# SwiGLU block products: weight sums formed by accumulating DMAs, another order of the 28 steps, unsplit value products, the last block by token tile

## The chip, the cores and the metric

One core of one Trainium2 chip runs one program, a whole decoder layer. The metric is the device time of one execution in microseconds (us). Names of the engines in the rows: PE is TensorE's matmul side and PEld its weight loads, DVE is VectorE, ACT is ScalarE, POOL is GpSimd, SP is SyncE, which here only issues transfers. SPq, ACTq and POOLq are the queues of DMA issues of those engines.

## What is computed

A layer on 512 tokens of width 2048, float32 in and out. The change touches the last two sublayers and one product of the first stage; the mixer ahead of them is left as it was.

```python
xa = _memory_cross_attention(h, mem, w_xq[l], w_xk[l], w_xv[l], w_xo[l])
h = _layer_norm(DEEPNORM_ALPHA * h + xa, ln2_g[l], ln2_b[l])
ff = (jax.nn.silu(h @ w_ffn_gate[l]) * (h @ w_ffn_up[l])) @ w_ffn_down[l]
h = _layer_norm(DEEPNORM_ALPHA * h + ff, ln3_g[l], ln3_b[l])
```

w_ffn_gate and w_ffn_up are 2048 x 5632, w_ffn_down is 5632 x 2048. The cross attention has 4 heads of 512 over 256 memory tokens.

## The kernel before, in words

**Precision.** A float32 product is made of three matmuls on rounded halves: a value x is stored as hi (x rounded to the matmul's type) and lo (x minus hi). hi is a cast on ACT, lo a subtract on DVE. Every weight tile goes through this pair once, every activation operand too.

**Seven products for eight.** The FFN runs as 2x2 block products by Strassen and Winograd's scheme, with 7 products P1 to P7 for 8. For gate and up there are 11 blocks j = 0 to 10 (512 output columns of gate and of up each): B11 and B21 are the two row halves of the gate columns, B12 and B22 those of the up columns, and the left operands are sums of quarters of the activations. For down there are 6 blocks: groups of 4, 4 and 3 of the gate/up blocks, two column halves each. A product is cut along the contraction into chunks c (4, or 3 in the last group), so a block has 28 steps, the last two blocks 21. One step (mm_item, L1298 to L1307) is 12 matmuls of 128x512 with one weight tile of 256x512.

**The feed of weights.** Class Feed prepares the weight tile of each step ahead of time. pump (L1142) lets SP load a 512 KB block tile into T0 to T3 or into one of four tiles rt. a (L1152 to L1154) subtracts two weight blocks on DVE where the product needs a sum (L1152), takes a tile ws (three of them) and casts the sum into its hi half on ACT (L1154). b (L1161) forms the lo half on DVE and frees the tiles that were used up. product_block calls after() behind each step: a for the step three ahead, b for the one two ahead, then pump. A block needs 20 loads of 512 KB and 16 subtracts at L1152 in gate/up.

**Order.** plan holds the order of the steps: P1 four times, P5 four times, then P6, P7, P3 for each chunk, then P2, P4 for each chunk. Each engine takes its instructions in the order in which the program issues them. Work beside the products (the elementwise part of a block, transposes, layer norms) is written as generators; sched advances them by one yield at each tick().

**Between blocks.** on() takes the products from PSUM with adds on DVE (L1333) and copies on ACT. ff_out transposes silu(gate)*up (L1342), forms the sums and differences for the down product (sums, L1040 to L1044; L1445 is the product ahead of the transposes), splits them (L1356 on ACT, L1360 on DVE) and sends them to comb_d in HBM by 16 small DMAs that ACT issues. load_comb brings them back for the down blocks.

**Ahead of the FFN.** wo_task (L534 to L539) multiplies the memory's values by w_xo; split_psum (L245, L246) splits each product into hi and lo, and POOL's DMA stores both to vo_d. At the output projection of the cross attention ("xo" below) next_w reloads the split halves as weights: whi and wlo, each by DMA. ln2 (L1010) and the transposes in first_half and second_half (L1053 in second_half) then build the seven activation operands. y2n_d keeps the normalised activations for the residual, which residual_task (L1293, L1294) turns into the term added behind the down product.

**The end.** In the last down block P4 is held back and done by token tile, so that final_ln (L1484 to L1493: DVE, ACT and POOL) can start on one tile while PE works on the next.

Of the kernel before, what the change touches and what calls it, by code (L numbers as in the profile page):

```python
# [9 lines left out]
F32 = mybir.dt.float32  # L10
F32R = mybir.dt.float32r
# [28 lines left out]
def layer_kernel(tc, x, mem, positions, ln_in_g, ln_in_b, w_in, sgu_norm_g, sgu_norm_b,  # L40
# [148 lines left out]
    def w_split(c):  # L189
# [192 lines left out]
    vo_d = [[dramp.tile([P, 2, 4, 512], F32R, name=f"vo_d{kb}_{cb}") for cb in range(4)] for kb in range(2)]  # L382
# [147 lines left out]
    def vo_chunk(h, cb):  # L530
        wh, wl = next_w(f"vo{h}_{cb}", 0)
        for mt in range(2):
# [440 lines left out]
    def zt(i, dt=F32):  # L973
        return pf[1].tile([P, 512], dt, name=f"z{i}")

    class Pieces:
        def __init__(self, where):
            self.t = {k: zt(i) for k, i in where.items()}

        def __getitem__(self, key):  # L980
            return self.t[key]
# [5 lines left out]
    comb_d = [dramp.tile([P, 7, 2, 256], F32R, name=f"comb_d{q}") for q in range(22)]  # L987
    comb = {}
    PS1, PS2, PS3, PS4, PA12, PA22, PA11 = range(7)

    def new_comb(p):
        if p == PA11 or p == PA12:
            comb[p] = [pf[0].tile([P, 4, 2, 256], F32R, name=f"c{p}_{h}") for h in range(2)]
        elif p == PS1 or p == PS2:
            comb[p] = [bigp.tile([P, 4, 2, 256], F32R, name=f"big{2 * (p == PS2) + h}") for h in range(2)]
        else:
            nm = {PS3: "wraw", PS4: "whi", PA22: "wlo"}[p]
            comb[p] = [wp.tile([P, 4, 2, 256], F32R, name=nm, bufs=2) for h in range(2)]

    def cslot(p, q, hl):  # L1000
        return comb[p][q // 4][:, q % 4, hl]
# [15 lines left out]
    def cm(i):  # L1017
        return pf[0].tile([P, 512], F32, name=f"cm{i}")

    def first_half():  # L1020
        for k in range(KT):
            p = aux()
            for t in range(2):
                T.transpose(p[:, t * 128:(t + 1) * 128], y2[t, k // 4][:, (k % 4) * 128:(k % 4) * 128 + 128], ident)
            g, b = cols[:, L2G + k:L2G + k + 1], cols[:, L2B + k:L2B + k + 1]
            pr = PA11 if k < 8 else PA12
            hi, lo = cslot(pr, k % 8, 0), cslot(pr, k % 8, 1)
            hf = cm(k % 4)[:, 0:256]
            A.activation(hi, p[:, 0:256], AF.Identity, bias=b, scale=g)
            if k % 2:  # L1030
                A.activation(hf, p[:, 0:256], AF.Identity, bias=b, scale=g)
            else:
                V.tensor_scalar(hf, p[:, 0:256], g, b, op0=OP.mult, op1=OP.add)
            V.tensor_tensor(lo, hf, hi.bitcast(F32), OP.subtract)
            if k % 2:
                yield 1

    def sums(xx, yy, ss, dd):
        a11, a21, a12, a22 = xx[:, 0:256], xx[:, 256:512], yy[:, 0:256], yy[:, 256:512]
        s1, s2, s3, s4 = ss[:, 0:256], ss[:, 256:512], dd[:, 0:256], dd[:, 256:512]  # L1040
        V.tensor_tensor(s1, a21, a22, OP.add)
        V.tensor_tensor(s2, s1, a11, OP.subtract)
        V.tensor_tensor(s3, a11, a21, OP.subtract)
        V.tensor_tensor(s4, a12, s2, OP.subtract)  # L1044
        return s1, s2, s3, s4

    def second_half():
        for q in range(8):
            m = []
            for n, k in enumerate((q, q + 8)):  # L1050
                p = aux()
                for t in range(NT):
                    T.transpose(p[:, t * 128:(t + 1) * 128], y2[t, k // 4][:, (k % 4) * 128:(k % 4) * 128 + 128],  # L1053
                                ident)
                g, b = cols[:, L2G + k:L2G + k + 1], cols[:, L2B + k:L2B + k + 1]
                m.append(cm(3 - n))
                A.activation(m[n], p, AF.Identity, bias=b, scale=g)
            ss, dd = cm(0), cm(1)
            s1, s2, s3, s4 = sums(m[0], m[1], ss, dd)
            src = ((PS1, s1), (PS2, s2), (PS3, s3), (PS4, s4), (PA22, m[1][:, 256:512]))  # L1060
            for pr, s in src:
                A.copy(cslot(pr, q, 0), s)
            for pr, s in src:
                V.tensor_tensor(cslot(pr, q, 1), s, cslot(pr, q, 0).bitcast(F32), OP.subtract)
            yield 1
        res_ready[0] = True


    class Feed:
        def __init__(self):  # L1070
            self.items, self.loads = [], []
            self.nl = self.na = self.nb = self.pos = 0
            self.rt = []
            self.T = {}

        def block(self, aps, n, order):
            T_, R = {}, {}
            base = len(self.items)

            def load(kind, c, tag, key):  # L1080
                self.loads.append((len(self.items), kind, aps[kind](c), tag, key))

            def add(name, c):
                e = dict(key=(name, c))
                if name == "P1":
                    load("B11", c, ("T", c), (base, "T", c))
                    e["src"] = (base, "T", c)
                elif name == "P5":
                    load("B12", c, ("r",), (base, "r5", c))
                    e["op"] = ((base, "T", c), (base, "r5", c), (base, "T", c))  # L1090
                    e["src"] = (base, "T", c)
                    e["free"] = [(base, "r5", c)]
                elif name == "P6":
                    load("B22", c, ("r",), (base, "r1", c))
                    e["op"] = ((base, "T", c), (base, "r1", c), (base, "T", c))
                    e["src"] = (base, "T", c)
                elif name == "P7":
                    load("B12", c, ("r",), (base, "r2", c))
                    e["op"] = ((base, "r2", c), (base, "r1", c), (base, "r2", c))
                    e["src"] = (base, "r2", c)  # L1100
                    e["free"] = [(base, "r2", c)]
                elif name == "P3":
# [503 lines left out]
```

## Time and profile before

| | us |
|---|---|
| three runs | 2755.64, 2749.66, 2753.16 |
| their median | 2753.16 |
| the profiled execution | 2757.52 |
| its span | 2755.8 |

| stage, us of the span | length | steps in it |
|---|---|---|
| the cross attention's keys, values and value products: 0 to 307.2 | 307.2 | |
| mixer, and the cross attention up to xo: 307.2 to 1182.5 | 875.3 | |
| xo with ln2: 1182.5 to 1305.5 | 123.0 | |
| gate/up block 0: to 1413.1 | 107.6 | 28 |
| gate/up blocks 1 to 10: to 2258.0 | 844.9 | 280 |
| first down block: to 2354.9 | 96.9 | 28 |
| next four down blocks: to 2657.8 | 302.8 | 105 |
| last down block: to 2729.4 | 71.6 | 21 |
| last layer norm: to 2755.8 | 26.4 | |

The profiled execution took 1.7 us more than its span and 4.4 us more than the median of the runs. PE is busy in 95% of the span, DVE in 68%, ACT in 39%, POOL in 4%; the granted clock is 0.98 of full speed over the whole.

### The profile page before, as it was taken

How to read it: one execution, taken by the hardware profiler on the slowest of the kernel's cores; microseconds unless marked ns; L12 is line 12 of the kernel's file. 1: busy time of each engine (PE TensorE's matmuls, PEld its weight loads, DVE VectorE, ACT ScalarE, POOL GpSimd, SP SyncE). 2: the span in 40 equal slices, each digit the busy share in tenths (PEclk: the TensorE clock that was granted, in tenths of full speed). 3: DMA queues.
4: the chain of work that ended last, by engine and by line, in shares of the span. 5: the costliest groups of instructions: out<-in, count | busy, mean ns of one | idle time of the engine just before them, and what ended most of it. 6: DMA issues, size and time to landing. Idle time of an engine off the chain costs nothing.

```text
span 2755.8 us, 32085 instructions
## 1 busy us (share of the span) xinstructions
PE 2609.4 (95%) x12453; PEld 2160.1 (78%) x12453; DVE 1869.7 (68%) x2520; ACT 1076.7 (39%) x1440; POOL 111.2 (4%) x141
## 2 busy tenths in 40 slices
PE   8999999999999999998899999999999998999994
PEld 8998888888888888876677777777777776878873
DVE  4777656463554366324788788887778777778888
ACT  4454333232331242202644444544445443333332
POOL 1311000000000010001100000000000000000004
PEclk9999999999999999999899999999999999999997
DMA  8879732323253234179465566555555687574642
GB/s 288 249 238 318 231 92 77 92 77 107 77 185 106 92 107 168 61 284 354 122 190 180 180 206 186 186 183 176 164 187 157 203 285 264 199 282 163 258 160 76
DMA packets 302040, 496.65 MB, mean 180 GB/s; under 512 B 17344, under 2 KB 111296, under 8 KB 299840
## 3 DMA queue, kind: packets, MB, share of 16 engines
q1 hardware_dynamic: 240048, 413.52, 45.1%
q10 hardware_dynamic: 46032, 47.46, 5.4%
q0 software_dynamic: 15808, 33.63, 3.8%
q8 instruction: 98, 1.61, 0.2%
q14 instruction: 54, 0.44, 0.0%
HBM read 412.22 MB, written 82.31 MB: 179 GB/s over the span
## 4 chain that ended last, share of the span: by engine, by line
PE 29%; DVE 13%; DMA 8%; ACT 3%; issue 3%; ACTq 1%; SPq 0%; DVEq 0%
PE acc L1306 6%; PE acc L1307 6%; PE acc L1305 6%; DVE ws L1161 4%; PE D L1306 3%; PE D L1307 3%; PE D L1305 3%; ACT ws L1154 2%; DVE T L1152 2%; DVE z L1333 2%; DMA comb_d<-z 2%; DMA wlo<-vo_d 1%; DMA rt<-in_w_ffn_gate_dram 1%; DVE z L1360 1%; DMA rt<-in_w_ffn_down_dram 1%
## 5 line engine op out<-in xcount | busy, mean ns | idle before, releaser
L1154 ACT CAST ws<-T 128x1024 fp32r<-128x1024 f32 x264 | 277.2, 1051 | 457.2 <-DVE T L1152 215.8
L205 DVE TENSOR_TENSOR wlo<-wraw,whi 128x1024 fp32r<-128x1024 f32 x226 | 267.1, 1223 | 219.5 <-ACT whi L204 219.5
L1161 DVE TENSOR_TENSOR ws<-T,ws 128x1024 fp32r<-128x1024 f32 x264 | 321.6, 1220 | 90.2 <-ACT ws L1154 88.3
L204 ACT CAST whi<-wraw 128x1024 fp32r<-128x1024 f32 x226 | 226.0, 1049 | 286.4 <-PE acc L242 175.0
L1161 DVE TENSOR_TENSOR ws<-rt,ws 128x1024 fp32r<-128x1024 f32 x198 | 240.9, 1220 | 77.4 <-ACT ws L1154 69.7
L1154 ACT CAST ws<-rt 128x1024 fp32r<-128x1024 f32 x198 | 205.4, 1052 | 186.7 <-PE acc L1307 66.2
L1152 DVE TENSOR_TENSOR T<-rt,T 128x1024 f32<-128x1024 f32 x198 | 241.0, 1217 | 9.7 <-DMA rt<-in_w_ffn_down_dram 9.7
L1306 PE MATMUL acc<-ws,big 128*128 128x512 f32 x528 | 214.8, 407 | 26.2 <-DVE ws L1161 25.7
L1305 PE MATMUL acc<-ws,big 128*128 128x512 f32 x528 | 212.5, 402 | 8.9 <-ACT ws L1154 6.7
L1306 PE MATMUL acc<-ws,c 128*128 128x512 f32 x512 | 203.1, 397 | 9.5 <-DVE ws L1161 8.4
L1307 PE MATMUL acc<-ws,big 128*128 128x512 f32 x528 | 210.0, 398 | 0.0
L1305 PE MATMUL acc<-ws,c 128*128 128x512 f32 x512 | 203.0, 397 | 0.8 <-ACT ws L1154 0.8
L240 PE MATMUL acc<-whi,act 128*128 128x512 f32 x512 | 201.2, 393 | 0.0
L1307 PE MATMUL acc<-ws,c 128*128 128x512 f32 x512 | 200.7, 392 | 0.0
L241 PE MATMUL acc<-wlo,act 128*128 128x512 f32 x512 | 199.4, 389 | 0.2 <-DVE wlo L205 0.2
L242 PE MATMUL acc<-whi,act 128*128 128x512 f32 x512 | 199.3, 389 | 0.0
L240 PE MATMUL acc<-act,whi 128*128 128x512 f32 x384 | 152.1, 396 | 0.0
L1306 PEld LDWEIGHTS acc<-ws,big 128*128 128x128 f32 x528 | 101.7, 193 | 62.0 <-DVE ws L1161 42.1
L242 PE MATMUL acc<-act,wlo 128*128 128x512 f32 x384 | 149.8, 390 | 0.0
L241 PE MATMUL acc<-act,whi 128*128 128x512 f32 x384 | 149.6, 390 | 0.0
L240 PE MATMUL acc<-memT,whi 128*128 128x256 f32 x432 | 125.4, 290 | 8.0 <-DVE vT L246 5.1
L1305 PEld LDWEIGHTS acc<-ws,big 128*128 128x128 f32 x528 | 101.5, 192 | 34.6 <-ACT ws L1154 10.1
(303 smaller groups left out, 5676.3 us busy)
## 6 DMA issues: line engine op xcount, KB each, us to landing
rt<-in_w_ffn_up_dram SPq DMA_DIRECT2D x132, 512.0 KB, 4.4
rt<-in_w_ffn_down_dram SPq DMA_DIRECT2D x88, 512.0 KB, 4.9
wraw<-in_w_in_dram SPq DMA_DIRECT2D x40, 1024.0 KB, 5.4
comb_d<-z ACTq DMA_DIRECT2D x132, 256.0 KB, 3.4
rt<-in_w_ffn_gate_dram SPq DMA_DIRECT2D x48, 512.0 KB, 4.8
T<-in_w_ffn_gate_dram SPq DMA_DIRECT2D x44, 512.0 KB, 3.8
wraw<-in_w_xv_dram SPq DMA_DIRECT2D x16, 1024.0 KB, 7.4
wraw<-in_w_xo_dram SPq DMA_DIRECT2D x16, 1024.0 KB, 6.6
```

Of the source, the lines that this page charges most:

```text
L204: A.copy(hi[s], r[:, z])
L205: V.tensor_tensor(lo[s], r[:, z], hi[s].bitcast(F32), OP.subtract)
L240: T.matmul(o, lh, rh, start=start, stop=False)
L241: T.matmul(o, lh, rl, start=False, stop=False)
L242: T.matmul(o, ll, rh, start=False, stop=stop)
L1152: V.tensor_tensor(o, x, y_, OP.subtract)
L1154: A.copy(e["ws"][:, 0], self.tiles[e["src"]])
L1161: V.tensor_tensor(e["ws"][:, 1], self.tiles[e["src"]], e["ws"][:, 0].bitcast(F32), OP.subtract)
L1305: T.matmul(banks[i], lh, rh, start=start and kk == 0, stop=False, skip_group_check=True)
L1306: T.matmul(banks[i], lh, rl, start=False, stop=False, skip_group_check=True)
L1307: T.matmul(banks[i], ll, rh, start=False, stop=kk == 1, skip_group_check=True)
L1333: V_ADD = lambda o, a_, b_: V.tensor_tensor(o, a_, b_, OP.add)
```

## The change

**Weight sums by DMA (gate/up).** Feed.block now gives each step a source tile and what is to happen to that tile behind the step's lo half ("post"). A tile X is loaded with B11 (gate) and serves P1; then POOL issues a DMA that adds B12 (up) onto it in place, and it serves P5; then one adds B22 (up) for P6, and one adds B21 (gate) for P4. Y is loaded with B22, serves P3, and gets B12 added for P7. Z is B21 for P2. So SP makes 12 loads of a block in place of 20, and POOL issues 16 accumulating DMAs of 512 KB. In the down blocks the sum for P6 is one DVE add for each chunk (the "add" in post), the rest is as in gate/up. Signs that the sums no longer carry are moved into the activation operands (L5, L6, L7, L3, A12, A22, A11).

**Order and ring.** Steps go by ORD; ws has four tiles; after() calls b ahead of a; on() comes behind after(). PSUM banks alternate in pairs. a is four steps ahead of PE's step, and b three ahead.

**Elementwise work in larger tiles.** to_features, ff_first and ff_second replace ff_out: casts and subtracts of 2 to 4 tiles of 512 at a time, comb_d stored by four DMAs of SP. residual_task runs in blocks 1 to 4. second_half goes by pairs with 32 transposes in place of 64, and block 0 waits for each chunk of the operands apart (gate). The operands of the next down group are loaded as each product of the block ahead ends.

**Value products unsplit.** wo_task copies the product to SBUF in float32 by one ACT copy, and POOL stores half the bytes; xo reloads one float32 tile of 1 MB in place of two split ones, and splits it like the other weights (2 casts of ACT and 2 subtracts of DVE for each of 16 chunks; L199 and the line behind it).

**Last block.** P7 and P4 stand last and go by token tile; tokens 0 and 1 are complete behind P6, step 15 of 21. The last two weight tiles of ws go into tiles of their own.

**The scratch of POOL's descriptors** is 1024 in place of 4096.

```diff
         def a(self):
...
-            if "op" in e:
-                o, x, y_ = (self.tiles[k] for k in e["op"])
-                V.tensor_tensor(o, x, y_, OP.subtract)
-            e["ws"] = pf[0].tile([P, 2, 1024], F32R, name="ws", bufs=NW)
+            if e["extra"]:
+                e["ws"] = pf[0].tile([P, 2, 1024], F32R, name=e["extra"])
+            else:
+                e["ws"] = pf[0].tile([P, 2, 1024], F32R, name="ws", bufs=NW)
             A.copy(e["ws"][:, 0], self.tiles[e["src"]])
...
             V.tensor_tensor(e["ws"][:, 1], self.tiles[e["src"]], e["ws"][:, 0].bitcast(F32), OP.subtract)
+            for act_ in e["post"]:
+                if act_[0] == "add":
+                    x_, y_ = self.tiles[act_[1]], self.tiles[act_[2]]
+                    V.tensor_tensor(x_, x_, y_, OP.add)
+                elif act_[0] == "acc":
+                    t = self.tiles[act_[1]]
+                    G.dma_start(t.rearrange("p (k c) -> p k c", k=2),
+                                act_[2].rearrange("(k p) c -> p k c", p=P), accum_op=OP.add)
...
         def after(self):
+            self.b()
             self.a()
-            self.b()
             self.pump()

-    NR, NW = 4, 3
+    NR, NW = 4, 4
...
+    head = lambda n: seq("P1", n) + seq("P2", n) + seq("P5", n)
+    ORD = {4: head(4) + its("30 60 31 61 32 33 62 70 63 71 72 73 40 41 42 43"),
+           3: head(3) + its("30 31 60 32 61 62 70 71 72 40 41 42")}
...
-            kv = p0.tile([P, 2, 512], F32R, name="vst", bufs=3)
-            split_psum(kv, p)
-            G.dma_start(vo_d[h // 2][cb][:, :, (h % 2) * 2 + mt], kv)
+            kv = p0.tile([P, 512], F32, name="vst", bufs=3)
+            A.copy(kv, p)
+            G.dma_start(vo_d[h // 2][cb][:, (h % 2) * 2 + mt], kv)
...
-    nc = _bacc.Bacc("TRN2", target_bir_lowering=False, num_devices=1, dynamic_dma_scratch_size=4096)
+    nc = _bacc.Bacc("TRN2", target_bir_lowering=False, num_devices=1, dynamic_dma_scratch_size=1024)
```

**Where instructions moved: the feed of a gate/up block.** DVE before, in the second half of a block: L1152 is a weight sum, L1161 a lo half, T2 and T3 are block tiles, rt the ring of four.

```order
L1161 TENSOR_TENSOR ws_14952<-rt_14815,ws_14952 128x1024
...
L1152 TENSOR_TENSOR rt_14907<-rt_14882,rt_14907 128x1024
L1161 TENSOR_TENSOR ws_14978<-T2_14611,ws_14978 128x1024
L1161 TENSOR_TENSOR ws_15000<-rt_14907,ws_15000 128x1024
L1152 TENSOR_TENSOR T3_14644<-rt_14955,T3_14644 128x1024
L1161 TENSOR_TENSOR ws_15015<-rt_14882,ws_15015 128x1024
L1152 TENSOR_TENSOR rt_14981<-rt_14955,rt_14981 128x1024
L1161 TENSOR_TENSOR ws_15041<-T3_14644,ws_15041 128x1024
L1161 TENSOR_TENSOR ws_15059<-rt_14981,ws_15059 128x1024
```

DVE now, in the middle of a block (L1166 is a lo half, L1323 an add out of PSUM):

```order
L1166 TENSOR_TENSOR ws_13093<-T0_12851,ws_13093 128x1024
L1166 TENSOR_TENSOR ws_13112<-T1_12872,ws_13112 128x1024
L1323 TENSOR_TENSOR Xa_13054<-D_10193,Xa_13054 128x512
L1323 TENSOR_TENSOR Xa_13054<-D_10194,Xa_13054 128x512
L1166 TENSOR_TENSOR ws_13130<-T2_12903,ws_13130 128x1024
L1166 TENSOR_TENSOR ws_13152<-T3_12922,ws_13152 128x1024
L1166 TENSOR_TENSOR ws_13168<-rt_13031,ws_13168 128x1024
L1166 TENSOR_TENSOR ws_13184<-T0_12851,ws_13184 128x1024
```

POOL now, in the same block; in the blocks of before its queue holds none of these:

```order
L1173 DMA T2_12903<-in_w_ffn_up_dram 128x2x512
L1173 DMA T3_12922<-in_w_ffn_up_dram 128x2x512
L1173 DMA rt_13031<-in_w_ffn_up_dram 128x2x512
L1173 DMA T0_12851<-in_w_ffn_gate_dram 128x2x512
L1173 DMA rt_13077<-in_w_ffn_up_dram 128x2x512
L1173 DMA T1_12872<-in_w_ffn_gate_dram 128x2x512
```

The weight sums are gone from DVE's row and stand in POOL's queue, each behind the lo half that last read its tile.

**ACT in xo.** Before, ACT has the normalisation (L1010) and first_half's work (L1029, L1031; c_0 and c_1 are operand tiles) in one run:

```order
L1010 ACTIVATE z_9520<-z_9520,mv 128x512
L1010 ACTIVATE z_9524<-z_9524,mv 128x512
L1010 ACTIVATE z_9521<-z_9521,mv 128x512
L1010 ACTIVATE z_9525<-z_9525,mv 128x512
L1029 ACTIVATE c_0_9796<-aux,cols 128x256 x2
L1031 ACTIVATE cm_9833<-aux,cols 128x256
```

Now (L199 is the cast of a value-product tile, L1016 the normalisation, L1040 and L1044 first_half):

```order
L199 CAST whi<-wraw 128x1024 x14
L1016 ACTIVATE Xb<-Xb,mv 128x512
L1016 ACTIVATE XH<-XH,mv 128x512
...
L199 CAST whi<-wraw 128x1024 x2
L1040 ACTIVATE Xb<-aux,cols 128x256 x2
L1044 CAST c_0_9763<-Xb 128x512
...
L199 CAST whi<-wraw 128x1024 x2
L1040 ACTIVATE Xb<-aux,cols 128x256 x2
```

The casts that make xo's weights now stand in ACT's queue between and behind the norm and first_half's work.

## Rows read from the trace of the kernel before

**Rows 1.** Stretches: start:end, length, busy of each engine (instructions), PEclk, DMA share, GB/s.

```profile
0.00:307.20 307.20, 290.11 (x2017) 272.19 (x2018) 204.04 (x288) 148.93 (x205) 50.30 (x73) 0.99 0.86 274
1182.52:1305.54 123.02, 107.07 (x474) 85.61 (x472) 41.41 (x95) 21.37 (x42) 7.29 (x12) 0.94 0.91 335
1305.54:1413.11 107.57, 94.52 (x402) 73.81 (x401) 87.62 (x150) 61.63 (x97) 8.34 (x12) 0.92 0.46 140
1413.11:2258.02 844.91, 806.15 (x3522) 644.86 (x3520) 686.95 (x768) 399.87 (x501) 0.00 (x0) 1.00 0.59 188
2258.02:2354.94 96.92, 84.08 (x354) 65.09 (x352) 71.62 (x82) 35.49 (x42) 0.00 (x0) 0.98 0.78 268
2354.94:2657.77 302.83, 293.13 (x1261) 237.69 (x1260) 240.24 (x243) 110.11 (x105) 0.00 (x0) 0.99 0.60 214
2657.77:2729.40 71.63, 61.94 (x253) 48.28 (x251) 65.55 (x84) 24.44 (x25) 9.56 (x7) 0.93 0.32 113
2729.40:2755.80 26.40, 0.16 (x1) 0.00 (x0) 22.54 (x32) 3.04 (x4) 18.24 (x14) 0.56 0.37 139
```

**Rows 2.** Waits of PE, then of ACT, in 1413.11:2258.02: us in total, times, longest.

```profile
PE acc L1306 <- DVE ws L1161: 20.9, 32, 1.4
PE aux L1342 <- DVE z L1445: 11.2, 20, 1.4
...
ACT ws L1154 <- DVE T L1152: 94.6, 42, 3.9
```

**Rows 3.** PE's timeline, one step of a gate/up block: start, length, [idle before, releaser].

```profile
1669.97 0.39 PE L1305 MATMUL acc<-ws,c 128*128 128x512 f32 x1
...
1672.69 0.38 PE L1342 MATMUL aux<-ident,z 128*128 128x128 f32 x2
1673.85 0.33 PE L1342 MATMUL aux<-ident,z 128*128 128x128 f32 x1 [0.78 <-DVE z L1445]
```

**Rows 4.** Groups by line and form in 1413.11:2258.02: busy us, mean ns, idle before.

```profile
L1161 DVE TENSOR_TENSOR ws<-T,ws 128x1024 fp32r<-128x1024 f32 x160 | 195.1, 1219 | 62.5 <-ACT ws L1154 61.0
L1152 DVE TENSOR_TENSOR T<-rt,T 128x1024 f32<-128x1024 f32 x120 | 146.1, 1217 | 0.0
L1152 DVE TENSOR_TENSOR rt<-rt 128x1024 f32<-128x1024 f32 x40 | 48.7, 1217 | 0.0
L1333 DVE TENSOR_TENSOR z<-D,z 128x512 f32<-128x512 f32 x40 | 27.5, 689 | 9.7 <-PE D L1307 9.2
...
L1154 ACT CAST ws<-T 128x1024 fp32r<-128x1024 f32 x160 | 168.0, 1050 | 242.6 <-DVE T L1152 94.6 <-PE acc L1307 66.1 <-DMA comb_d<-z 57.6
```

**Rows 5.** DMA in 1413.11:2258.02: a queue's packets, MB, share; issues, KB each, us to landing.

```profile
q1 hardware_dynamic: 63725, 121.81, 45.2%
...
rt<-in_w_ffn_up_dram SPq DMA_DIRECT2D x116, 512.0 KB, 4.5
```

**Rows 6.** POOL's issue of the vo_d stores, then (whole run) their landing.

```profile
L539 POOL DMA_DIRECT2D vo_d<-vst x32: 684/685/793, 76.4 to 312.3; - x32
```
```profile
vo_d<-vst POOLq DMA_DIRECT2D x32, 512.0 KB, 7.8
```

**Rows 7.** Wait for ACT at the vo_d split, PE's waits in xo, first L1010.

```profile
ACT vst L245: 21.8, 6
```
```profile
PE acc L241 <- DMA wlo<-vo_d: 13.6, 8, 4.4
```
```profile
1246.12 0.81 ACT L1010 ACTIVATE z<-z,mv 128x512 f32<-128x512 f32 x1 [48.87 <-DVE mv L390]
```

**Rows 8.** Waits of PE in block 0.

```profile
PE aux L1053 <- ACT cm L1057: 8.3, 5, 2.8
```

**Rows 9.** Timelines of DVE, POOL and PE in the last down block.

```profile
2717.92 0.22 DVE L272 SCALAR_TENSOR_TENSOR rs_c<-mv,rs_c 128x1 f32<-128x1 f32 x1
...
2718.37 1.18 DVE L272 SCALAR_TENSOR_TENSOR rs_c<-mv,rs_c 128x1 f32<-128x1 f32 x1
```
```profile
2718.27 1.26 POOL L1488 TENSOR_TENSOR z<-z,c 128x512 f32<-128x512 f32 x1 [1400.56 <-ACT z L1487]
```
```profile
2722.47 0.80 PE L1306 MATMUL D<-ws,wlo 128*128 128x512 f32 x1 [4.47 <-DVE ws L1161]
```

More of the change, by code (lines that the diff above doesn't have):

```diff
@@ L1015, in ln2, with hcol @@
                 G.dma_start(y2n_d[t][c], y2[t, c])
-    def cm(i):
-        return pf[0].tile([P, 512], F32, name=f"cm{i}")
+    def hcol(k):
+        return cols[:, L2G + k:L2G + k + 1], cols[:, L2B + k:L2B + k + 1]
     def first_half():
[L1021 to L1036, printed above, removed]
@@ L1072, in __init__, with block @@
             self.nl = self.na = self.nb = self.pos = 0
[L1073 to L1077, printed above, removed]
+            self.tiles = {}
+            self.live_r = 0
+            self.live_T = set()
+        def block(self, aps, n, order, dma_t2):
             base = len(self.items)
[L1080 to L1084, printed above, removed]
+            for name, c in order:
+                X, Y, Z = (base, "T", c), (base, "Y", c), (base, "Z", c)
+                e = dict(key=(name, c), post=[], extra=None)
+                at = len(self.items)
@@ L1199, in layer_kernel @@
                "B22": lambda c, z=z: half_rows(w_up, 1024 + 256 * c, z)}
[L1200 to L1205 removed]
+        plan.append((4, ORD[4]))
+        feed.block(aps, 4, ORD[4], True)
     for g, n in enumerate((4, 4, 3)):
@@ new lines, in to_features, with ff_first @@
+    def to_features(fc, x, slots):
+        ps = []
+        for n in range(2):
+            p = aux()
+            ps.append(p)
+            for kk in range(2):
+                f = 2 * n + kk
+                for i in range(2):
+                    T.transpose(p[:, kk * 256 + i * 128:kk * 256 + i * 128 + 128], x[:, i, f * 128:f * 128 + 128],
+                                ident)
+        yield 1
+        for n in range(2):
+            A.copy(fc[:, slots[n]], ps[n])
+    def ff_first(j, fc, x12):
+        yield from to_features(fc, x12, (A11, A12))
@@ L1528, in on @@
                 elif name == "P7":
                     for i in range(2):
[L1530 to L1539 removed]
+                        acc_y(2 + i, n1, bk[i], last)
@@ new lines, in layer_kernel @@
+            if last and nb:
+                cut = [o for o in order if o[0] in ("P7", "P4")]
+                bank = product_block(n, order[:-len(cut)], on)
+                ws = []
+                for name in ("P7", "P4"):
+                    ws = [None] * n
+                    for i in range(2):
+                        for c in range(n):
+                            if ws[c] is None:
+                                ws[c] = feed.next((name, c))
+                            mm_item(bank[name], COMB[name], c, ws[c], c == 0, c == n - 1, (i,))
+                            if name == "P7" and i == 0:
+                                feed.after()
+                                feed.after()
+                            tick()
+                        t = 2 + i
+                        if name == "P7":
+                            acc_y(t, n1, bank[name][i], True)
+                            acc_y(t, n0, bank[name][i])
+                        else:
+                            acc_y(t, n0, bank[name][i], True)
+                            sched.spawn(final_ln(t), 1)
```

610 lines of the change are left out of this document (296 added, 314 removed).

## The prediction

> **What bounds the kernel now.** I read the stretches first, to see where time is lost that the change can reach. In the gate/up and down blocks PE is near its floor [rows 1]: a step lasts 2.72 us from its first matmul to the transpose behind it (1669.97 to 1672.69) [rows 3], so 28 steps need 76.2 us and 21 need 57.1. Blocks 1 to 10 take 844.9 us, 84.5 each, 8.3 over the steps; the first down block is 20.7 over its steps, the next four (105 steps, 285.6) are 17.2 over together, the last is 14.5 over [rows 1]. Of a block's 8.3, the 16 transposes take some 2.5 (an estimate: two in a row start within 0.4, [rows 3]), 3.9 is idle time of PE (844.9 less 806.2 over ten blocks, [rows 1]), and the rest is matmuls that are busy for longer than their turn.
>
> The waits say who ends the idle time: the lo half on DVE (20.9 us), then DVE's product ahead of the transposes (11.2) [rows 2]. ACT in turn stood 94.6 us for the weight sums of DVE [rows 2]. DVE is busy for 687.0 of 844.9 us [rows 1], 68.7 a block; 160 of its instructions there are weight sums, 194.8 us or 19.5 a block [rows 4]. So PE's floor bounds these blocks, and the chain DVE sum, ACT cast, DVE lo adds the loss on top.
>
> **Part 1: the sums leave DVE.** Now a block has on DVE 28 lo halves of 1.22 (34.2), 8 adds out of PSUM of 0.69 (5.5) [rows 4], and by the diff some 10 us of products, combinations and subtracts that I cost by elements from the same 0.69 for 512. That is about 50 us of 76, and each lo half waits for a cast alone. What goes: the 20.9 of waits and the stretched matmuls. What stays: 2.5 for transposes, and about 1.6 for waits such as the 11.2 and the few on ACT [rows 2], since the product still stands ahead of the transposes. A block is then 76.2 + 2.5 + 1.6 = 80.3, ten blocks 803, a gain of 42. If all waits went it would be 57 (78.7 a block); if none of the idle time went, 19 (the 1.9 of stretch alone).
>
> The cover: 16 accumulating DMAs a block lie beside PE. The trace has none, so their price is bounded. As a plain copy, 512 KB costs 1.64 us of the 16 engines (45.2% of 844.9 for 121.81 MB, [rows 5]), and POOL's software queue costs the same per byte (3.8% of 2755.8 for 33.63 MB, [rows 6]). A block then moves 12 loads, 7 units of 512 KB for comb_d and 16 accumulates, 35 units: 57 us of engine time in 80. An accumulate also reads what stands in the tile; if that doubles it the block has 51 units, 84 us at 1.64, or 73 at the 1.42 of xo (335 GB/s at a share of 0.91, [rows 1]). If read, read and write all count it is 67 units, 95 to 110. Below 1.64 nothing can come, as the bytes are the same. I take the lower end, but between one and two units, since loads of the trace are nearest in kind; both ends stay in the range.
>
> Latency: between P5 and P6 of the same chunk lie at least five steps. b runs three ahead and the cast four ahead, so an accumulate that is issued behind one lo half has about four steps, 10.9 us, until ACT wants the tile. A store of POOL's queue landed 7.8 us after its issue, in a stretch with DMA at 0.86, and the issue takes POOL 0.68 [rows 1, 6]: 8.5 in all, which fits. In these blocks POOL has nothing else, busy 0.00 [rows 1], so 16 issues of 0.68 (10.9 us) cost it nothing that anyone waits for. ACT is where a late accumulate would show: the cast stands there, and behind it in order are PSUM copies and the next casts; PE has three prepared tiles, 8.2 us, before it feels it.
>
> **Part 2: order and ws of four.** One more tile ahead gives PE 2.72 us of slack more, against waits whose longest was 1.4 [rows 2]. It is counted in the 42.
>
> **Part 3: block 0 and second_half.** Block 0 lasts 107.6, 31.4 over its steps [rows 1]. Halving the transposes saves 32 of about 0.16, 5 us, and PE waited 8.3 for ACT's operand [rows 8]. Its 16 accumulates are new, and the operands are still made inside it, DVE being busy for 87.6 [rows 1]. I take 7, between 0 and 15.
>
> **Part 4: xo.** It lasts 123.0 with DMA at a share of 0.91 [rows 1]. PE waited 13.6 us for wlo to come back [rows 7]. Half the reload bytes end that. New are 32 casts (1.05 each) and 32 subtracts (1.22) [rows 4]: 33.6 us on ACT and 39.0 on DVE, which with 21.4 and 41.4 [rows 1] still fit into 123. But ACT takes its work in order: the casts of two chunks now stand behind the four normalisations of 0.81 each, and these wait for DVE's statistics [rows 7]. I charge 3.6 for that (four of 0.81, and a little): gain 10, between 0 (PE waits for the casts as it did for the tiles) and 17 (the clock of 0.94 recovers too). In the first stage POOL stores half the bytes, and the 21.8 that ACT stood for a free vst [rows 7] goes; PE is busy there for 290.1 of 307.2 [rows 1], so little is to be had: 3.
>
> **Part 5: down blocks.** The first loses 20.7 with DMA at 0.78 [rows 1], where operand loads meet weight loads. Loading operands as each product of block 10 ends, and the loss of DVE work (12 sums of a block become accumulates, 4 stay as adds), should give 12 of it, and 5 of the 17.2 behind: 17, between 5 and 28.
>
> **Part 6: the last block and the norm.** Together 98.0 us [rows 1]. PE stood 4.47 us for a lo half [rows 9]: it was queued on DVE behind final_ln's short operations, one of which took 1.18 in place of 0.22 while POOL multiplied beside it [rows 9]. The two tiles of their own let P4's halves be made before that. Tokens 0 and 1 end at step 15 of 21 (18 before). The tail of tokens 2 and 3 stays. I take 7, between 3 and 12.
>
> **The sum** against the profiled execution: 42 + 7 + 10 + 3 + 17 + 7 = 86, 2757.5 - 86 = 2671.5. That execution is 4.4 above the median of the three, so the forecast is **2667 us**, 3.1% less. By the bounds of the parts it is 19 + 0 + 0 + 0 + 5 + 3 = 27 to 57 + 15 + 17 + 3 + 28 + 12 = 132, that is 2726 to 2621.
>
> **The rivals.**
>
> *The DMA engines become the bound.* An accumulate takes two units or nearly. 51 units are 73 to 84 us, and since the share was never above 0.91 in a stretch [rows 1], a block lasts 80 to 92. At 86, blocks 0 to 10 lose 5.7 each, 63 us: 2667 + 63 = 2730; with the ends 2667 to 2790. For it: DMA sits at 0.59 in these blocks and the accumulates replace loads of as many bytes, so even a modest surcharge brings it to 0.8. Against: at 0.78 to 0.91 PE still ran at 87% [rows 1]. The Trainium skill has a rule that speaks for it: "Collectives: The Full Stack", section "The bandwidth ceiling: the fold count and why AG ≠ RS ≠ AR", says that an add in the DMA path needs two source reads on the same ring, and that it ran at 32.35 GB/s where the copy ran at 62.28. By that ratio of 1.93 an accumulate would cost 3.2 us of the engines here, and a block 82 us of engine time. No row of this case shows it.
>
> *Slower: the accumulates go one after another.* All 16 of a block go through POOL's one queue, with a quarter of the descriptor scratch. If each must land before the next is issued, one takes 0.68 + 4.5 (a load's landing, [rows 5]) to 0.68 + 7.8 [rows 6], 5.2 to 8.5. At 6.5 a block of gate/up lasts 104, 24 more than forecast, eleven blocks 261: 2930. It decides from 5.5 us each: 16 of those are 88, which uses up the gains elsewhere. For it: the scratch is smaller, and nothing in the trace shows POOL with two such transfers close together, as its issues in the first stage are spread over 236 us for 32 [rows 6]. Against: 8.5 is a latency, and transfers of SP's queue overlap, 116 loads of 4.5 beside others [rows 5]. The Trainium skill, "DMA: Bandwidth & Descriptors", section "Anatomy of one DMA — SWDGE (gpsimd) path", gives 2.0 us and the bytes over 436 GB/s for one such transfer. By it one takes an estimated 3.2 us, and 16 in a row 51 us, which would not bind; the vo_d row [rows 6] is longer than that.
>
> *No change.* The wait for DVE's sum turns into ACT's wait for the accumulate, of the same size, with PE still at 84.5 a block, and ACT's order in xo eats the 13.6. Then the rest gives 0 to 10: about 2750. Against: the accumulates have four steps of lead, the sums had none.
>
> **How the numbers follow.** Forecast 0.50 (2621 to 2726), DMA-bound 0.24 (2667 to 2790), one after another 0.20 (2800 and more), no change 0.06. A measurement of this kernel can tell 0.2%, 5.5 us, from no change. Of DMA-bound a sixth, 0.04, ends above 2758. So faster is 0.50 + 0.20 = 0.70, same 0.06, slower 0.24. The range leaves out the serial case and a little at the low end: 2630 to 2780.
>
> **What would show it.** Right: blocks 1 to 10 at 79 to 82 us each, DVE near 50 us a block, no wait of PE for a lo half above 1 us, DMA share 0.65 to 0.85, the time from an accumulate's issue to its landing below 10 us. DMA-bound: the share near 0.9 in the blocks, ACT waiting for the accumulated tiles, loads of SP landing after 8 us and more. One after another: DMA share low while ACT waits for tiles, and POOL's issues spaced by the landing of the one ahead. Xo right: at 110 to 116 us with no wait for a DMA of vo_d; wrong if PE waits there for L199 or the line behind it. The forecast is wrong outright if an accumulate takes above 3 us of the engines.

## The result, and the profile after

The changed kernel took 3250.25 us (median of four runs, 3243.07 to 3253.38) against 2751.95 of the kernel before: 1.181 times as long, interval 1.178 to 1.183. The forecast was 2667, so it was wrong in sign; the rival that it gave 0.20, accumulates one after another, is what happened, and it cost more than the 2930 us that it gave.

The stages of the kernel after, in the columns of [rows 1], row for row the same eight stages:

```profile
0.00:297.00 297.00, 287.40 (x2017) 269.63 (x2018) 186.93 (x259) 150.50 (x206) 45.78 (x74) 1.00 0.79 259
1171.81:1288.11 116.30, 103.30 (x473) 83.99 (x472) 70.09 (x109) 51.68 (x72) 8.60 (x13) 0.96 0.58 202
1288.11:1416.33 128.22, 96.64 (x378) 74.36 (x377) 67.01 (x95) 56.73 (x78) 27.84 (x28) 0.88 0.61 124
1416.33:2667.46 1251.13, 950.97 (x3522) 724.46 (x3521) 503.16 (x482) 385.24 (x420) 193.10 (x160) 0.85 0.71 166
2667.46:2767.98 100.52, 85.38 (x345) 67.29 (x344) 57.53 (x59) 33.92 (x33) 14.45 (x12) 0.93 0.80 218
2767.98:3146.24 378.26, 319.00 (x1262) 250.21 (x1260) 196.34 (x208) 106.24 (x104) 54.35 (x46) 0.91 0.75 193
3146.24:3222.60 76.36, 63.33 (x253) 49.89 (x251) 49.53 (x66) 23.80 (x25) 22.02 (x16) 0.91 0.60 136
3222.60:3250.10 27.50, 0.18 (x1) 0.00 (x0) 23.47 (x39) 3.04 (x4) 17.39 (x13) 0.60 0.33 124
```

Against [rows 1], up to the FFN 17.4 us are gained (it starts at 1288.1 in place of 1305.5). Then block 0 loses 20.7, blocks 1 to 10 lose 406.2 (125.1 a block in place of 84.5), the first down block 3.6, the next four 75.4, the last 4.7 and the norm 1.1. Together that is the 494.3 by which the span grew. Every block of the FFN, where the accumulating DMAs run, is longer; of the stages without them only the last norm is, by its 1.1. In blocks 1 to 10 no engine is near its limit in the mean: PE 76%, DVE 40%, DMA 0.71, where [rows 1] had 95%, 81% and 0.59.

The waits in blocks 1 to 10 name the chain. First ACT's, then PE's, then POOL's (us in total, times, longest):

```profile
ACT ws L1159 <- DMA rt<-in_w_ffn_up_dram: 400.0, 40, 15.1
ACT ws L1159 <- DMA T<-in_w_ffn_up_dram: 259.6, 48, 12.3
```
```profile
PE D L1297 <- ACT ws L1159: 145.7, 37, 7.5
PE acc L1297 <- ACT ws L1159: 72.0, 27, 8.2
```
```profile
POOL T L1173 <- issue: 495.5, 77, 13.1
```

PE waits for ACT's cast. The cast waits for a tile that an accumulate fills: only POOL moves rows of up into T tiles, and the waits for rt end some 6.3 us behind an accumulate's issue, as for the last one of POOL's lines below:

```profile
1738.50 1.04 ACT L1159 CAST ws<-rt 128x1024 fp32r<-128x1024 f32 x1 [11.84 <-DMA rt<-in_w_ffn_up_dram]
```

POOL, which issues the accumulates, waits for nothing that the profile can name ("issue"). Its timeline in one block (start, length, idle before) shows the rhythm:

```profile
1706.73 1.20 POOL L1173 DMA_DIRECT2D T<-in_w_ffn_up_dram  x1 [11.01 <-issue]
1713.17 1.22 POOL L1173 DMA_DIRECT2D T<-in_w_ffn_up_dram  x1 [5.24 <-issue]
1719.49 1.20 POOL L1173 DMA_DIRECT2D T<-in_w_ffn_up_dram  x1 [5.11 <-issue]
1725.79 1.22 POOL L1173 DMA_DIRECT2D T<-in_w_ffn_up_dram  x1 [5.10 <-DVE ws L1166]
1732.16 1.20 POOL L1173 DMA_DIRECT2D rt<-in_w_ffn_up_dram  x1 [5.16 <-issue]
```

In these lines one accumulate is issued every 6.3 to 6.4 us. The list of issues gives the time from issue to landing:

```profile
rt<-in_w_ffn_up_dram POOLq DMA_DIRECT2D x40, 512.0 KB, 6.1
```

So each is issued as soon as the one ahead has landed. The start and the landing of every accumulate in the trace say it outright. Of the 160 in blocks 1 to 10, 150 start 0.32 us after the landing of the one ahead, and in the whole run none starts while another is under way. Ten times, at the start of a block, POOL waits for a lo half instead, until 4.7 to 6.1 us behind the landing. These parts make up the stage: 1151 us with one accumulate under way, 48 us of such 0.32 and 52 us of those ten waits are its 1251.

The mean from issue to landing is 7.2 us and the median 6.2. Some five accumulates of a block, those around its start, take more than 7 us (up to 13.9); SP's loads of the block run then, and the DMA engines are full. The first line below is such a start (DMA share 0.97), the second the rest of the same block (0.54):

```profile
1665.00:1707.00 42.00, 31.97 (x139) 25.08 (x139) 23.11 (x23) 17.93 (x19) 5.10 (x5) 0.94 0.97 297
1707.00:1779.00 72.00, 51.05 (x163) 37.78 (x164) 21.57 (x21) 17.22 (x20) 13.44 (x12) 0.77 0.54 80
```

The granted clock is 0.85 in these blocks (1.00 in [rows 1]); it falls behind PE's idle stretches:

```profile
1707.61 0.80 PE L1297 MATMUL acc<-ws,big 128*128 128x512 f32 x1 [8.17 <-ACT ws L1159]
```

Behind this one PE's matmuls start 0.43 us apart and later 0.23, about the ratio of its two levels, 1.2 and 2.4 GHz, and the step begun there takes 5.5 us in place of 2.72. That lengthens PE's work, but it is a result of the waits and not what sets the block: 1199 of the 1251 us are POOL's transfers one behind the other.

The queues in the same stretch (packets, MB, share of the 16 engines):

```profile
q0 software_dynamic: 43520, 83.90, 42.8%
q1 hardware_dynamic: 50735, 122.78, 27.9%
```

An accumulate of 512 KB cost the engines 0.428 x 1251.13 / 83.90 x 0.524 = 3.35 us, a load of SP's queue 1.49.

### The profile page after: what moved, and what is told of

Read it like the earlier page. It is cut to its first block, busy times and chain, and to the rows that moved or that the text cites. A ratio compares the mean times of both kernels' runs of the same rounds, so it can differ in the third digit from the quotient of the medians.

```text
span 3250.1 us, 31768 instructions
## 1 busy us (share of the span) xinstructions
PE 2778.1 (85%) x12421; PEld 2252.6 (69%) x12421; DVE 1603.3 (49%) x2095; ACT 1084.4 (33%) x1364; POOL 399.6 (12%) x383
## 4 chain that ended last, share of the span: by engine, by line
issue 40%; DMA 9%; POOL 6%; DVE 4%; PE 2%; ACT 1%; SPq 0%; POOLq 0%; ACTq 0%; DVEq 0%
POOL T L1173 4%; DMA rt<-in_w_ffn_up_dram 2%; DMA T<-in_w_ffn_down_dram 2%; POOL rt L1173 2%; DVE ws L1166 1%; DMA T<-in_w_ffn_gate_dram 1%; DMA r_d<-FH 1%; DMA Xa<-res_d 1%; ACT ws L1159 1%; DMA wraw<-vo_d 1%; PE acc L1298 1%; PE acc L1299 0%; PE acc L1297 0%; DVE wlo L200 0%; DVE XH L1323 0%
## 5 line engine op out<-in xcount | busy, mean ns | idle before, releaser
L1166 DVE TENSOR_TENSOR ws<-T,ws 128x1024 fp32r<-128x1024 f32 x262 | 315.2, 1222 | 441.0 <-ACT ws L1159 441.0
L1166 DVE TENSOR_TENSOR ws<-rt,ws 128x1024 fp32r<-128x1024 f32 x198 | 242.0, 1225 | 519.3 <-ACT ws L1159 518.7
L1159 ACT CAST ws<-T 128x1024 fp32r<-128x1024 f32 x262 | 270.0, 1049 | 644.0 <-DMA T<-in_w_ffn_up_dram 259.6
L200 DVE TENSOR_TENSOR wlo<-wraw,whi 128x1024 fp32r<-128x1024 f32 x258 | 304.6, 1223 | 271.4 <-ACT whi L199 267.9
L199 ACT CAST whi<-wraw 128x1024 fp32r<-128x1024 f32 x258 | 257.9, 1048 | 336.7 <-PE acc L237 192.2
L1297 PE MATMUL D<-ws,wraw 128*128 128x512 f32 x264 | 141.6, 536 | 185.3 <-ACT ws L1159 185.1
L1297 PE MATMUL acc<-ws,big 128*128 128x512 f32 x528 | 224.5, 425 | 68.7 <-ACT ws L1159 68.7
L1298 PE MATMUL acc<-ws,big 128*128 128x512 f32 x528 | 225.2, 426 | 21.6 <-DVE ws L1166 21.6
L1297 PEld LDWEIGHTS D<-ws,wraw 128*128 128x128 f32 x264 | 67.5, 256 | 226.3 <-ACT ws L1159 211.5
L1299 PE MATMUL acc<-ws,big 128*128 128x512 f32 x528 | 219.8, 416 | 0.0
L1173 POOL DMA_DIRECT2D T<-in_w_ffn_up_dram x88 | 106.3, 1208 | 722.1 <-issue 352.5
L1297 PEld LDWEIGHTS acc<-ws,big 128*128 128x128 f32 x528 | 109.4, 207 | 105.0 <-ACT ws L1159 81.2
L1298 PE MATMUL D<-ws,wraw 128*128 128x512 f32 x264 | 142.2, 539 | 33.3 <-DVE ws L1166 33.3
L1297 PE MATMUL acc<-ws,whi 128*128 128x512 f32 x264 | 113.2, 429 | 40.7 <-ACT XH L1424 32.8
L1298 PEld LDWEIGHTS acc<-ws,big 128*128 128x128 f32 x528 | 108.5, 206 | 56.1 <-DVE ws L1166 32.9
```

Source lines behind the costliest of these rows:

```text
L199: A.copy(hi[s], r[:, z])
L200: V.tensor_tensor(lo[s], r[:, z], hi[s].bitcast(F32), OP.subtract)
L1159: A.copy(e["ws"][:, 0], self.tiles[e["src"]])
L1166: V.tensor_tensor(e["ws"][:, 1], self.tiles[e["src"]], e["ws"][:, 0].bitcast(F32), OP.subtract)
L1173: G.dma_start(t.rearrange("p (k c) -> p k c", k=2), act_[2].rearrange("(k p) c -> p k c", p=P), accum_op=OP.add)
L1297: T.matmul(bank[i], lh, rh, start=start and kk == 0, stop=False, skip_group_check=True)
```

## Experiments

Theory A: POOL's scratch for descriptors, 1024 bytes, has room for one accumulate of 512 KB and not for two, so POOL cannot issue the next until the one ahead has landed. Theory B: accumulates of one queue run one after another whatever the scratch. A third possibility is that the DMA engines are full. All the kernels below are the changed one with the edit shown. The last column is the most accumulates (in halves, half accumulates; in copy, copies) that the trace has under way together.

| kernel | median us | blocks 1 to 10, us each | under way at most |
|---|---|---|---|
| before | 2751 to 2752 | 84.5 | none |
| changed | 3250.25 | 125.1 | 1 |
| s1280 | 2701.6 | 83.5 | 2 |
| s1088 | 2704.7 (one run) | 83.5 | 2 |
| s1728 | 2693.5 | 82.1 | 3 |
| halves | 2738.1 (one run) | 86.2 | 3 |
| copy | 2636.0 (one run) | 78.0 | 3 |
| t2dve | 3020.6 | 103.8 | 1 |
| alldve | 2699.0 | 80.4 | none |
| t2s1728 | 2656.3 | 78.6 | 3 |
| t2s1088 | 2655.8 | 78.2 | 2 |
| t2y | 2648.1 | 78.7 | 3 |

**s1280**

```diff
-dynamic_dma_scratch_size=1024
+dynamic_dma_scratch_size=1280
```

> The changed kernel with the descriptor scratch at 1280 in place of 1024, nothing else. Theory A (POOL cannot issue an accumulate until the one ahead has landed, because the scratch holds the descriptors of one and not of two): the distance between accumulates that are queued back to back falls from 6.4 us to about 3.4 us, what one costs the DMA engines (42.8% of 1251 us for 83.9 MB is 3.35 us for 512 KB), blocks 1 to 10 take 85 to 95 us instead of 125, the time is 2800 to 2900 us. Theory B (accumulates of one queue run one after another in any case): distance 6.4 us and 3250 us as before.

Measured: 2701.63 us, 0.982 of before (0.979 to 0.985), 549 us less than with 1024, and better than the 2800 to 2900 that A expected. POOL's timeline in a block, then blocks 1 to 10, then the queues in them:

```profile
1691.04 1.19 POOL L1173 DMA_DIRECT2D rt<-in_w_ffn_up_dram  x1 [1.75 <-issue]
1694.37 1.22 POOL L1173 DMA_DIRECT2D T<-in_w_ffn_gate_dram  x1 [2.14 <-issue]
1697.30 1.20 POOL L1173 DMA_DIRECT2D rt<-in_w_ffn_up_dram  x1 [1.71 <-issue]
1700.66 1.22 POOL L1173 DMA_DIRECT2D rt<-in_w_ffn_up_dram  x1 [2.17 <-issue]
```
```profile
1385.85:2221.12 835.27, 802.58 (x3521) 654.05 (x3520) 502.33 (x482) 387.67 (x419) 191.72 (x160) 0.98 1.00 245
```
```profile
q0 software_dynamic: 43518, 83.89, 59.1%
q1 hardware_dynamic: 49360, 120.14, 40.2%
```

The distance is 3.2 us in the mean (9.62 over three). These accumulates still land 6.1 us after their issue (median of their groups; those of up onto T took 10.7), so two are under way. B falls. The issue itself takes POOL 1.21 us with either scratch, so the time was not in issuing. Now the DMA engines are full: 59.1% and 40.2% make 99%, and an accumulate costs 0.591 x 835.27 / 83.89 x 0.524 = 3.08 us of them. The 835.27 is ten blocks at 83.5: with the scratch out of the way the DMA engines are full in these blocks, at almost no gain over the 84.5 before.

**copy** leaves the adding out: the same bytes go down the same queue as plain copies.

```diff
-act_[2].rearrange("(k p) c -> p k c", p=P), accum_op=OP.add)
+act_[2].rearrange("(k p) c -> p k c", p=P))
```

> The changed kernel with the accumulating DMAs made plain copies of the same bytes on the same queue (the adding is left out), scratch at 1024. Theory A (scratch): a copy reads one stream and not two and needs fewer descriptors, so more than one is under way, the distance falls to 2 us or less and blocks 1 to 10 take 78 to 84 us; total 2660 to 2720 us. Theory B (one after another whatever they are): the distance is the landing time of a copy, 4 to 5 us, blocks near 95 us, total about 2900 us. If an accumulate is serial because it adds, copies overlap too, and only the run with more scratch tells it from A.

Measured: 2636.04 us (one run). POOL's issues, one group, and its timeline in a block; blocks 1 to 10; POOL's queue:

```profile
L1173 POOL DMA_DIRECT2D rt<-in_w_ffn_up_dram x44: 704/707/727, 1337.6 to 2139.1; - x44
```
```profile
1663.18 0.71 POOL L1173 DMA_DIRECT2D rt<-in_w_ffn_up_dram  x1 [1.50 <-DVE ws L1166]
1664.40 0.72 POOL L1173 DMA_DIRECT2D T<-in_w_ffn_gate_dram  x1 [0.51 <-issue]
1665.64 0.71 POOL L1173 DMA_DIRECT2D rt<-in_w_ffn_up_dram  x1 [0.52 <-issue]
```
```profile
1391.80:2171.31 779.51, 779.51 (x3521) 647.14 (x3520) 508.12 (x482) 395.99 (x419) 114.07 (x160) 1.00 0.76 265
```
```profile
q0 software_dynamic: 23062, 83.99, 31.5%
```

With the scratch still at 1024, copies overlap: these three start 1.2 us apart, and each landed 4.7 to 5.2 us after its issue. PE is busy for all of the 779.5 us and waits for nothing. An accumulate costs the engines 3.08 us against 1.53 for a copy, two transfers for one; its issue takes POOL 1.21 us against 0.71, 1.7 times as long. The run also makes 77.95 us the floor of a block in this order.

**s1088**

```diff
-dynamic_dma_scratch_size=1024
+dynamic_dma_scratch_size=1088
```

> The changed kernel with the scratch at 1088. If the limit is a count of descriptors, then one step above 1024 decides it. An estimate by the Trainium skill, DMA: Bandwidth & Descriptors, section The descriptor swizzle (16 engines, one completion descriptor on each side) and its 16-byte descriptors: 512 KB in rows of 2 KB is 16 rows on each engine, read twice 32 and one more, so 33; two are 66; 1024 bytes hold 64 and 1088 hold 68. By this the run is like the one at 1280, 2690 to 2720 us. If the limit lies elsewhere between 1024 and 1280, it is like the changed kernel, 3250 us.

Measured: 2704.7 us (one run), blocks 1 to 10 at 834.8 us. So 64 bytes of scratch are worth 546 us, and the step lies between 1024 and 1088. The expectation's estimate, from the Trainium skill, "DMA: Bandwidth & Descriptors", section "The descriptor swizzle", gave 66 descriptors for two accumulates, between the 64 and the 68 that the two sizes hold. Descriptors are counted in no profile, but the trace agrees with what follows from that estimate: by it one accumulate fits at 1024, two at 1088 and 1280, three at 1728, and (17 descriptors each) three copies or three half accumulates at 1024. That is the last column of the table.

**halves**

```diff
-G.dma_start(t.rearrange("p (k c) -> p k c", k=2),
-            act_[2].rearrange("(k p) c -> p k c", p=P), accum_op=OP.add)
+for kk in range(2):
+    G.dma_start(t[:, kk * 512:kk * 512 + 512], act_[2][kk * P:kk * P + P], accum_op=OP.add)
```

> The changed kernel with each accumulate of 512 KB issued as two of 256 KB, scratch at 1024. Theory A: two or three halves fit the scratch together, so the landing of one lies beside the transfer of the next; a pair takes 4 to 5 us in place of 6.4, blocks 95 to 105 us, total 2950 to 3050 us. Theory B: a half takes its own 4 to 5 us of latency, a pair 9 us, blocks 150 us or more, total above 3500 us.

Measured: 2738.13 us (one run), better than A expected: blocks at 86.2. The scratch is at 1024 here, and three halves are under way together, so smaller pieces end the serial order by themselves. DMA is at 0.98 in the blocks, near the 1.00 of s1280.

**s1728**

```diff
-dynamic_dma_scratch_size=1024
+dynamic_dma_scratch_size=1728
```

> The changed kernel with the scratch at 1728: room for three accumulates. If the 86 us blocks among blocks 1 to 5 of the run at 1280 still lack accumulates under way, they fall to 80 us and the total to about 2680 us. If the DMA engines bind there (16 x 3.35 us and the loads are about 84 us), the time stays at 2700 us.

Measured: 2693.48 us, 0.978 of before (0.976 to 0.980). Blocks 1 to 10:

```profile
1389.21:2210.32 821.11, 795.63 (x3522) 653.05 (x3520) 503.24 (x480) 391.40 (x418) 190.22 (x158) 0.99 0.98 248
```

A third accumulate under way brings 8 us over s1280, between the two expectations; the slow blocks stay (87.2 and 84.7 among the first five, 91.3 the last). DMA is full at 0.98. It is the engines and no longer the scratch. The 4096 bytes of before were not tried with the change.

**t2dve and t2s1728.** P6's sum goes back to DVE, 12 accumulates a block in place of 16; the second with the scratch at 1728.

```diff
-feed.block(aps, 4, ORD[4], True)
+feed.block(aps, 4, ORD[4], False)
```

> The changed kernel with P6's sum in gate/up made by a DVE add per chunk, as its down blocks already do, so that a block has 12 accumulates in place of 16; scratch at 1024. If the queue of accumulates sets the block (16 x 6.4 us = 102 us and the waits around it), a block loses about 4 x 6.4 = 26 us, 99 in place of 125, total about 2970 us. If it is the 73 to 84 us of DMA engine time that binds, it loses 4 x 3.35 = 13 us a block and the total is about 3100 us. If DVE is the bound it gets slower by 5 us a block.

> Scratch at 1728 and P6's sum by DVE add, 12 accumulates a block. DMA engine time falls by 4 x 3.35 = 13 us a block to some 70 us, DVE rises by 4 x 1.22 = 5 us to some 55. If the DMA engines were what held the run at 1280 above the copy run (77.95 us a block), blocks 1 to 10 take 78 to 80 us and the total is 2640 to 2660 us. If DVE matters, above 2700 us.

Measured: 3020.61 us at 1024 and 2656.28 us at 1728, 0.965 of before (0.963 to 0.967). At 1024 accumulates still go one at a time, and a block is 103.8 us, 21.3 less: between the 13 of DMA time and the 26 of the serial queue, and nearer to the latter. Blocks 1 to 10 of t2s1728:

```profile
1386.77:2172.69 785.92, 782.10 (x3521) 648.10 (x3519) 549.57 (x520) 394.94 (x418) 141.93 (x118) 1.00 0.89 232
```

DMA has room again (0.89), and eight of the ten blocks stand at 77.97, the floor that copy showed. DVE rose to 55.0 us a block, and in the ten blocks PE waited for it 0.8 us in all. Both limits were real: the scratch first, the DMA engines behind it.

**alldve.** No accumulates: the second operand is loaded by SP into a ring of six rt tiles (ws back at three) and added by DVE behind the lo half. The added loads are left out of the edit below.

```diff
...
-elif act_[0] == "acc":
...
+elif act_[0] == "sum":
+    x_, y_ = self.tiles[act_[1]], self.tiles.pop(act_[2])
+    V.tensor_tensor(x_, x_, y_, OP.add)
+    self.live_r -= 1
...
-NR, NW = 4, 4
+NR, NW = 6, 3
```

> No accumulating DMA at all in gate/up and down: SP loads the second operand into the ring of rt (six tiles, ws back at three for the space) and DVE adds it behind the lo half, in the changed order; all other parts of the change stay. DVE then has about 70 us a block again, as before. If the wait for DVE's sums set the 84.5 us of before, blocks stay at 83 to 85 us and the total is 2690 to 2720 us. If the order (add behind the lo half, steps ahead of its cast) was what mattered and the engine that adds did not, blocks take 78 to 80 us and the total is 2640 to 2670 us.

Measured: 2699.04 us, 0.981 of before (0.979 to 0.982). Blocks 1 to 10 and PE's waits in them:

```profile
1392.69:2197.16 804.47, 787.51 (x3522) 646.85 (x3521) 692.35 (x642) 397.28 (x420) 0.00 (x0) 1.00 0.68 230
```
```profile
PE acc L1304 <- DVE ws L1172: 13.7, 11, 1.3
```

DVE is busy for 692 us, as much as before (687), and a block takes 80.4 (79.7 in nine of ten). So of the 6.5 us a block between before and copy, 4.0 came without any sum leaving DVE, with the order (the sum stands behind a lo half, steps ahead of its cast), the larger tiles of the elementwise work and the longer ring of rt. At most 2.5 came by taking the sums off DVE. The total misses the expected 2640 to 2670. Against t2s1728 the blocks 1 to 10 are 18.6 longer in all, the four down blocks in the middle 13.7 and the last 15.1 (82.3 us). In the last, PE stood 10.2 and 7.3 us for single lo halves of DVE; whether DVE's added work or the ring of ws at three is behind it was not tried.

**t2y and t2s1088** both have 12 accumulates a block. t2y is t2s1728 with one more edit, t2s1088 is t2s1728 with the scratch at 1088. In t2s1728 the first down block took 99.3 us. PE's wait there, and DVE's timeline ahead of it:

```profile
PE D L1298 <- DVE ws L1166: 13.2, 1, 13.2
```
```profile
2206.02 1.36 DVE L1521 TENSOR_TENSOR Xa<-Xa,acc 128x512 f32<-128x512 f32 x2 [11.17 <-DMA Xa<-r_d]
2207.30 1.75 DVE L1374 TENSOR_TENSOR FC<-FC,XH 128x1536 f32<-128x1536 f32 x1
2208.97 1.22 DVE L1166 TENSOR_TENSOR ws<-rt,ws 128x1024 fp32r<-128x1024 f32 x1
```

DVE stands for residual rows that SP issued only at 2194.9 and that took 11.0 us to land, and the lo half that PE wants is queued behind. t2y loads them earlier:

```diff
             elif name == "P7":
+                if j == FB - 1:
+                    load_y("Xa", [(0, 0), (1, 0)])
...
-        load_y("Xa", [(0, 0), (1, 0)])
```

> The 12-accumulate kernel with the scratch at 1728, and the residual rows of tokens 0 and 1 for the first down block loaded behind P7 of block 10, ahead of the operand loads in SP's queue. In the run without this, DVE stood 11.2 us in the first down block for these rows, with the lo halves of the next steps behind it, and PE lost 13.2 us. If that wait is the loss, the first down block goes from 99.3 to 86 to 90 us and the total to about 2645 us. If the block is bound by the DMA engines (busy 0.98 there), the operand loads come later by as much and the time stays at 2656 us.

> The 12-accumulate kernel with the scratch at 1088, room for two accumulates and not three. If two under way are enough once there are 12 a block, it gives 2656 us like the one at 1728; if the third carries the blocks, 2680 to 2700 us.

Measured: t2y 2648.14 us, 0.963 of before (0.960 to 0.965), the fastest of the kernels here that do every sum; its first down block is

```profile
2173.39:2262.49 89.10, 83.32 (x344) 68.12 (x345) 61.01 (x62) 36.40 (x35) 16.79 (x14) 0.92 0.99 288
```

10.2 us shorter, and DVE's adds no longer wait for the rows. t2s1088 gave 2655.83 us: with 12 accumulates a block, two under way are as good as three.

## Why the prediction was wrong

**Part 1, the cover: failed.** The step was "8.5 in all, which fits". It held one accumulate's latency against the four steps of its lead and never multiplied by 16 what the queue takes from one to the next. The diff showed the scratch cut to a quarter while 512 KB accumulates were put on that queue; it was named, and then weighed only as a rival. In its place the runs showed one accumulate under way at a time, 0.32 us between a landing and the next issue, and with 64 bytes more of scratch 546 us less. The signs that the prediction had named for this rival came true: a low DMA share while ACT waits for tiles, and issues spaced by the landing of the one ahead. The rival's distance of 6.5 us was right for most of a block. The block came to 125 and not 104 because the mean distance was 7.5, with the slow landings around a block's start (16 of 7.5 are 120), and because POOL waits there for a lo half once (5.2).

**The argument against the rival: failed.** "Transfers of SP's queue overlap" was true of SP's queue. POOL's overlaps as well, as far as the scratch holds what is under way (copy). The kernel before had shown it, at 4096 bytes. The prediction read there that no two of POOL's transfers stood close together, since 32 stores spread over 236 us, but they come in bunches:

```profile
292.72 0.69 POOL L539 DMA_DIRECT2D vo_d<-vst  x1 [1.77 <-DVE vst L246]
295.94 0.69 POOL L539 DMA_DIRECT2D vo_d<-vst  x1 [2.53 <-DVE vst L246]
298.96 0.69 POOL L539 DMA_DIRECT2D vo_d<-vst  x1 [2.34 <-DVE vst L246]
```

They are some 3 us apart and none of the 32 landed in less than 4.8 us, so up to three were under way. That spoke against a queue that is serial by nature, and it left open what a quarter of the scratch would do, which no row of before could tell.

**The price of an accumulate: mis-sized.** Between one and two units it took the lower end. It measured 3.08 us in s1280 and 3.35 in the changed kernel (2.89 in s1728) against 1.53 for a copy on the same queue, two units. That is above the 3 us at which the prediction called itself wrong outright. "Below 1.64 nothing can come" fell as well: a copy took 1.53 and SP's load 1.49. The ratio of 1.93 that the prediction quoted from the Trainium skill, "Collectives: The Full Stack", section "The bandwidth ceiling: the fold count and why AG ≠ RS ≠ AR", agrees with the 2.01 of s1280 over copy. With two units, the DMA-bound rival's block of 80 to 92 us came true in s1280 (83.5 at a DMA share of 1.00), though that kernel is not the one that was forecast. The prediction's other estimate, 3.2 us for one transfer by the Trainium skill, "DMA: Bandwidth & Descriptors", section "Anatomy of one DMA — SWDGE (gpsimd) path", does not agree: an accumulate took 6.1 us and more from issue to landing here, and the measurement decides.

**The size of the prize: right, in other kernels.** PE's floor of a block was put at 78.7 with no waits and 80.3 with some; copy showed 77.95, t2s1728 78.6. DVE was put at 50 us a block and has 50.3 (503.16 over ten).

**Xo and the first stage: right in sum, with the parts exchanged.** Forecast 10 and 3; measured 6.7 (123.0 to 116.3) and 10.2 (307.2 to 297.0). In place of the 13.6 for wlo [rows 7] PE waited for

```profile
PE acc L236 <- DVE wlo L200: 6.2, 5, 2.8
PE aux L1034 <- ACT Xb L1016: 5.2, 1, 5.2
```

which are the waits for the split and for the norm that the charge of 3.6 stood for, at three times the size. In the first stage PE's waits fell from 17.0 to 9.4 us, most of it waits for DVE's vT (5.1 to 0.5), while DVE, which no longer splits the products, is busy for 17.1 us less (204.0 to 186.9). The prediction had looked at ACT's wait alone. Whether the one follows from the other was not tried.

**Block 0, down blocks, the end: right in sum, and the down blocks by luck.** Behind the serial queue they can't be read in the changed kernel. In s1280, with nothing but the scratch altered, they are

```profile
1287.28:1385.85 98.57, 85.44 (x377) 69.12 (x376) 67.07 (x95) 57.41 (x78) 27.73 (x28) 0.97 0.79 170
2221.12:2316.39 95.27, 79.64 (x345) 64.68 (x344) 58.15 (x60) 35.34 (x34) 15.52 (x13) 0.93 0.93 261
2316.39:2605.34 288.95, 287.03 (x1262) 236.24 (x1260) 196.05 (x207) 108.26 (x104) 54.20 (x45) 1.00 0.94 249
2605.34:2672.70 67.36, 59.24 (x253) 48.17 (x251) 55.39 (x70) 23.94 (x25) 26.05 (x19) 0.95 0.68 168
2672.70:2697.10 24.40, 0.18 (x1) 0.00 (x0) 20.44 (x36) 3.04 (x4) 13.11 (x10) 0.61 0.29 107
```

Block 0 gained 9.0 (forecast 7), the first five down blocks 15.5 (17), the last block and the norm 6.3 (7). But the first down block gained 1.7 of its 12, and the four behind it 13.9 in place of 5. What the prediction missed in the first is the wait for residual rows: PE stood 13.5 us there in s1280, as in t2s1728, and without it (t2y) the block takes 89.1, 7.8 less than before.

So the sum was wrong by 583 us. Of these 549 were the scratch (s1280). Of the 35 that are left, 32 lie in blocks 1 to 10 of s1280 (83.5 in place of 80.3), where the accumulates fill the DMA engines. What the order, the ring and the larger tiles are worth apart from each other was not tried. Two of the prediction's sums are a little off and change nothing: the gain with all waits gone is 58 and not 57, and the upper end of the DMA-bound rival 2796 and not 2790.

## What to carry to other kernels

Before work moves to a queue that was nearly idle, ask what that queue can have under way, and multiply its distance from issue to issue by the number of transfers; a latency that fits one transfer's lead is no proof for sixteen. A DMA that adds costs the engines as much as two copies, and here it also filled the scratch where copies of the same bytes overlapped. When the engine that issues transfers waits for "issue" and each issue follows a landing, enlarge its descriptor space or cut the transfers into pieces before changing anything else. A sum of parts that comes out right says little of the parts: look at each stage by itself.

## What the runs showed of the hardware

The step in the scratch is sharp: 3250 us at 1024 bytes, 2705 at 1088, 2702 at 1280, 2693 at 1728. With one accumulate under way the 16 DMA engines are busy for 0.71 of blocks 1 to 10 while PE idles; with two they are full at 1.00. At 1024 bytes 217 of the 242 accumulates of the run start 0.32 us after the landing of the one ahead. Issuing an accumulate of 512 KB took POOL 1.21 us, a copy 0.71. POOL's queue moved 272 packets for an accumulate (43520 over 160) and 144 for a copy of the same bytes (23062 over 160).
